# One Trainium2 block kernel: h in a pool of its own, the first residues of pairs on older bytes, h's last squares ahead of its transposes, the third columns' end made prompt

## The chip, the cores and the metric

The kernel runs on one core of one Trainium2 chip. The metric is device time in microseconds (us) of one execution; lower is better. The core has four engines that matter here: TensorE (PE) for matmuls, VectorE (DVE), ScalarE (ACT) and GpSimd (POOL); SyncE (SP) issues most DMAs. Each engine runs its own list of instructions strictly in order. An instruction whose input isn't ready holds up all that stands behind it on that engine.

## What is computed

One layer over 256 tokens of 2048 features: attention heads and a convolution side by side, one output projection that adds into h, then a gated feed-forward network (FFN) that adds into the result. The part around the change is the end of the projection and the start of the FFN:

```python
    mixed = jnp.concatenate([att, u], axis=-1)
    h = h + jnp.einsum('bsm,md->bsd', mixed, w_out[l].astype(mixed.dtype))
    hn = rms_norm(h, norm2_g[l])
    a = jnp.einsum('bsd,df->bsf', hn, w_gate[l].astype(hn.dtype))
    bu = jnp.einsum('bsd,df->bsf', hn, w_up[l].astype(hn.dtype))
    h = h + jnp.einsum('bsf,fd->bsd', jax.nn.silu(a) * bu, w_down[l].astype(hn.dtype))
```

## The kernel before

Products run in a reduced format at float32 accuracy: each operand is the sum of a rounded high part (`hi`) and a residue (`lo`), and a product is made of three matmuls: high by high, residue of the activations by high part of the weights, high part by residue of the weights. For every chunk of weights, SP loads `raw` (512 KB), ACT casts it to `whi` (line 330), and DVE subtracts to get the residue `wlo` (line 339); for some chunks a POOL DMA makes the residue instead. PE uses the high parts first and the residues last.

The program is written as a list of chunks. For each chunk the loads, casts and residues of chunks some places ahead are issued, then its matmuls (`multiply`). What follows a group of chunks (adding a finished sum into h, transposing, normalizing) is written as generators: `multiply` calls `resume()` at fixed places, and each call takes every running generator to its next `yield`. So the number of `yield`s decides behind which chunk's work an instruction stands on its engine. A chunk with `prompt` gets one more `resume()` right after its matmuls if it ends a group.

The output projection has four blocks of 512 columns, n = 0 to 3. The first three are computed with interleaved chunks, and the fourth follows alone. At the end of block n, `out_done(n)` runs: DVE adds the two accumulators into h (line 848, one for each 128 tokens), PE transposes those columns into `ps_h` (line 861), ACT and DVE turn them into `hn` (line 865) or into `chi` and `clo` (870, 872), ACT takes the sums of squares (`h_squares`, line 493), and POOL stores h to DRAM (`h_store`, line 833). "Third columns" are n = 2, "last columns" n = 3. After n = 2, `make_forms` prepares the sums `fhi` and `flo` for the FFN.

The FFN has two kinds of units. Ordinary chunks use `chi` and `clo`. "Pairs" take four weight tiles `wb`, form sums `wt` of them (lines 1038 to 1040; on POOL for the first pair, on DVE for most others), cast both into `wh` (lines 1033, 1055), and take residues `wlb` and `wlt` (line 1062); PE multiplies them by seven products at lines 1078 to 1080.

SBUF is given out by pools that are stacked from both ends. On the right side stand `edge`, `keep` (the two tiles of h, the mixed activations, `junk` for the squares) and `small` (scalars for each row, `rsq` among them). When the last columns are done, `keep` and `small` are closed and the pool `late` takes their bytes: the residues `wlb` and `wlt`, the FFN's sums `sum0` to `sum3`, and others. A tile in `late` waits for whatever last read or wrote the bytes below it.

Of the kernel before, what the change touches and what calls it, by code (L numbers as in the profile page):

```python
# [12 lines left out]
F32 = mybir.dt.float32  # L13
F32R = mybir.dt.float32r
AF = mybir.ActivationFunctionType
ALU = mybir.AluOpType
AX = mybir.AxisListType

P = 128
D = 2048  # L20
S = 256
NM = S // P
# [9 lines left out]
N = 512  # L32
# [3 lines left out]
EPS = 1e-6  # L36
# [95 lines left out]
def tile_block(  # L132
# [6 lines left out]
    act, dve, pool, pe, sp = nc.scalar, nc.vector, nc.gpsimd, nc.tensor, nc.sync  # L139

    const = ctx.enter_context(tc.tile_pool(name="const", bufs=1))
# [4 lines left out]
    prestack, keepstack = ExitStack(), ExitStack()  # L146
    ctx.enter_context(tc.tile_pool(name="edge", bufs=1, side="right")).tile([P, EDGE // 4], F32, tag="edge", name="edge")
    keep = keepstack.enter_context(tc.tile_pool(name="keep", bufs=1, side="right"))
    small = keepstack.enter_context(tc.tile_pool(name="small", bufs=4, side="right"))
    pre = prestack.enter_context(tc.tile_pool(name="pre", bufs=2))  # L150
    acc_ps = ctx.enter_context(tc.tile_pool(name="acc", bufs=4, space=PSUM))
    aux_ps = ctx.enter_context(tc.tile_pool(name="aux", bufs=AUX, space=PSUM))


    h = [keep.tile([P, D], F32, tag=f"h{m}", name=f"h{m}") for m in range(NM)]
    away = ctx.enter_context(tc.tile_pool(name="away", bufs=1, space=bass.MemoryType.DRAM))
    hd = [away.tile([P, D], F32, tag=f"hd{m}", name=f"hd{m}") for m in range(NM)]

# [18 lines left out]
    def col(key, k):  # L177
        return cols[:, AT[key] + k : AT[key] + k + 1]
# [41 lines left out]
        pool.tensor_tensor(neg_lam, le[:, 1:2], le[:, 0:1], ALU.subtract)  # L220
        pool.tensor_scalar(neg_lam, neg_lam, 1.0, -LAMBDA_INIT, ALU.mult, ALU.add)

    def rsqrt_mean(dst, ss, n, eps):

        k = dst.shape[-1]
        t = small.tile([P, 8], F32, tag="rsq", name="rsq")
        pool.tensor_scalar(t[:, :k], ss, 1.0 / n, eps, ALU.mult, ALU.add)
        pool.tensor_tensor(dst, t[:, :k], neghalf[:, :k], ALU.pow)

# [37 lines left out]
    def room(n, hold=0):  # L267
        while held[0] + n > AUX:
            yield
        held[0] += hold  # L270


    side = []
# [21 lines left out]
    chunks = []  # L295
    before = {}

    def block(w, cols, ks, xs, done=None, bkey=None, first=True, last=True, spare=False, cuts=()):

        ks = list(ks)  # L300
        cols = [(cols, N)] if isinstance(cols, int) else cols
        width = sum(n for _, n in cols)
        bkey = bkey if bkey is not None else ("b", len(chunks))
        i = 0
        cuts = list(cuts)
        while i < len(ks):
            part = ks[i : i + (cuts.pop(0) if cuts else NK * N // width)]
            i += len(part)
            chunks.append(dict(w=w, ks=part, k0=part[0], nk=len(part), cols=cols, width=width, xs=xs, bkey=bkey,
                               first=part[0] == ks[0] and first, last=last and i == len(ks),  # L310
                               done=done if i == len(ks) else None, spare=spare, by_dma=False,
                               rows=slice(part[0], part[-1] + 1), load=load_chunk, round=round_chunk,
                               split=split_chunk, multiply=multiply))
# [177 lines left out]
    def square_sum(src, accum, **kw):  # L491
        junk = keep.tile([P, N], F32, tag="junk", name="junk")
        act.activation(junk[:, : src.shape[-1]], src, AF.Square, accum_out=accum, **kw)
# [333 lines left out]
    ss2 = [const.tile([P, 4], F32, tag=f"ss2_{m}", name=f"ss2_{m}") for m in range(NM)]  # L827
    rstd2s = const.tile([P, NM], F32, tag="rstd2", name="rstd2")
    rstd2 = [rstd2s[:, m : m + 1] for m in range(NM)]

    def h_store(cs):
        for m in range(NM):
            pool.dma_start(out=hd[m][:, cs], in_=h[m][:, cs])

    def h_squares(n, cs):
        for m in range(NM):
            square_sum(h[m][:, cs], ss2[m][:, n : n + 1])

    def out_done(n, ps):
        if not n:  # L840
            prestack.close()
            ffn["pool"] = fp = ctx.enter_context(tc.tile_pool(name="ffn", bufs=1))
            ffn["rows"] = fp.tile([P, 2, NS, S], F32, tag="wh", name="hn", bufs=2)
            for t in ("chi", "clo"):
                ffn[t] = fp.tile([P, len(REST), S], F32R, tag=t, name=t)
        cs = slice(n * N, (n + 1) * N)
        for m in range(NM):
            dve.tensor_tensor(h[m][:, cs], h[m][:, cs], ps[m], ALU.add)
        if n == 2:
            held[0] -= NM  # L850
        if n == D // N - 1:
            h_store(cs)
            yield
        yield
        for t in range(0, N // P, 2):
            k = n * (N // P) + t
            yield from room(1)
            pt = aux_ps.tile([P, 2, S], F32, tag="aux", name="ps_h")
            for i in range(2):
                for m in range(NM):  # L860
                    pe.transpose(pt[:, i, m * P : (m + 1) * P], h[m][:, (k + i) * P : (k + i + 1) * P], ident)
            if k % HK < NS:
                rows = ffn["rows"][:, k // HK, k % HK : k % HK + 2, :]
                for i in range(2):
                    act.activation(rows[:, i, :], pt[:, i, :], AF.Copy, scale=col("g2", k + i))
            else:
                a = REST.index(k)
                hi, lo = (ffn[x][:, a : a + 2, :] for x in ("chi", "clo"))
                for i in range(2):
                    act.activation(hi[:, i, :], pt[:, i, :], AF.Copy, scale=col("g2", k + i))  # L870
                for i in range(2):
                    dve.scalar_tensor_tensor(lo[:, i, :], pt[:, i, :], col("g2", k + i), hi[:, i, :].bitcast(F32),
                                             ALU.mult, ALU.subtract)
                    plain[k + i] = (hi[:, i, :], lo[:, i, :])
            yield
        h_squares(n, cs)
        if n < D // N - 1:
            h_store(cs)
        if n == HK * P // N:
            yield  # L880
            start(make_forms())
        if n == D // N - 1:
            yield
            ss = small.tile([P, NM], F32, tag="ssh", name="ssh")
            for m in range(NM):
                dve.tensor_reduce(ss[:, m : m + 1], ss2[m], AX.X, ALU.add)
            rsqrt_mean(rstd2s, ss, D, EPS)
            keepstack.close()
            ffn["late"] = ctx.enter_context(tc.tile_pool(name="late", bufs=1, side="right", reuse_waits="tile"))


    ffn = {}
# [409 lines left out]
    for ks, first, last in ((range(0, 4), True, False), (range(4, 8), False, False), (range(8, 16), False, True)):  # L1302
        for n in range(3):
            block(w_out, n * N, ks, fm, (lambda ps, n=n: out_done(n, ps)) if last else None,
                  bkey=("o", n), first=first, last=last, spare=n == 2)
    block(w_out, 3 * N, range(16), fm, lambda ps: out_done(3, ps))
    chunks[-1]["prompt"] = True
    for i, c in enumerate(chunks[OPENING:-12]):
# [67 lines left out]
```

## Time and profile before

| what | value |
|---|---|
| time, median of 3 runs | 1033.14 us (1032.98 to 1033.17) |
| the profiled execution's own time | 1033.09 us |
| its span in the profile | 1031.3 us |
| DMA moved in the span | 239.71 MB, mean 232 GB/s |
| granted TensorE clock | 1.0 |
| first add into h of the last columns (DVE) | 340.48 us after the span's start |
| first residue of a pair, `wlb` (DVE) | 348.53 us |
| first use of `wlt` (PE) | 352.62 us |

A row of a timeline has the start in us from the span's start, the length, the engine, the line of the kernel, the operation, output and inputs, shapes and count, and in brackets how long the engine idled before it and what ended that. PEld is PE's loading of weights, which runs beside its matmuls.

### The profile page before, as it was taken

What the parts mean: (1) busy time and instruction counts of PE and PEld (TensorE: products, weight loads), DVE (VectorE), ACT (ScalarE), POOL (GpSimd) and SP (SyncE); (2) the same over time, 40 slices, a digit from 0 to 9 for tenths busy, and PEclk for the clock granted to TensorE, in tenths of its full rate; (3) what the DMA queues carried; (4) which work ended last, traced back from release to release, by engine and by line L of the source; (5) the groups of instructions that cost most, each with busy time, mean ns of one, the idle gap of its engine ahead of it and who ended that gap; (6) DMA issues with size and microseconds to landing.
All of it is one profiled execution on the core that took longest, in us unless ns stands there. A gap on an engine that the chain in (4) does not pass through costs nothing.

```text
span 1031.3 us, 13149 instructions
## 1 busy us (share of the span) xinstructions
PE 1023.3 (99%) x4628; PEld 845.4 (82%) x4628; DVE 905.7 (88%) x1160; ACT 668.4 (65%) x863; POOL 185.1 (18%) x193
## 2 busy tenths in 40 slices
PE   9999999999999999999999999999999999999998
PEld 7888888888887778888888888888888888888887
DVE  6899999999756999899988897888989888789897
ACT  7644656665756676777765657677777556767662
POOL 0300112110002100212304212123022231220320
PEclk9999999999999999999999999999999999999999
DMA  9757555545457777987989899889798989797776
GB/s 336 261 189 263 186 184 164 164 163 174 165 191 247 238 226 211 295 268 211 251 261 233 274 286 246 264 239 234 250 276 237 264 228 305 229 259 228 232 189 176
DMA packets 116738, 239.71 MB, mean 232 GB/s; under 512 B 7872, under 2 KB 9152, under 8 KB 116672
## 3 DMA queue, kind: packets, MB, share of 16 engines
q1 hardware_dynamic: 105216, 203.58, 58.7%
q0 software_dynamic: 11168, 35.13, 18.1%
q8 instruction: 36, 0.59, 0.2%
q14 instruction: 30, 0.25, 0.1%
q10 hardware_dynamic: 288, 0.16, 0.1%
HBM read 204.24 MB, written 9.44 MB: 207 GB/s over the span
## 4 chain that ended last, share of the span: by engine, by line
PE 95%; DVE 2%; DMA 1%; issue 0%; SPq 0%; ACT 0%; POOL 0%; DVEq 0%; POOLq 0%; ACTq 0%
PE q L1099 11%; PE q L1100 11%; PE q L1105 11%; PE q L1080 10%; PE acc L375 10%; PE q L1078 10%; PE q L1079 10%; PE acc L369 9%; PE acc L370 9%; PE ps_a L906 1%; DMA wb<-in_w_gate_dram 1%; DMA raw<-in_w_in_dram 1%; DVE wlt L1062 1%; PE ps_s L726 1%; PE ps_o L796 1%; DVE wlb L1062 0%
## 5 line engine op out<-in xcount | busy, mean ns | idle before, releaser
L330 ACT CAST whi<-raw 128x1024 fp32r<-128x1024 f32 (+1 forms) x248 | 257.3, 1044 | 191.0 <-issue 86.4
L339 DVE TENSOR_TENSOR wlo<-raw,whi 128x1024 fp32r<-128x1024 f32 (+1 forms) x198 | 239.2, 1216 | 45.3 <-ACT whi L330 44.9
L1062 DVE TENSOR_TENSOR wlt<-wt,wh 128x1024 fp32r<-128x1024 f32 x130 | 153.0, 1218 | 16.3 <-ACT wh L1055 16.3
L1055 ACT CAST wh<-wt 128x1024 fp32r<-128x1024 f32 x130 | 132.9, 1051 | 41.7 <-DVE wt L1038 28.9
L1099 PE MATMUL q<-whi,chi 128*128 128x512 f32 x352 | 137.8, 391 | 0.0
L1100 PE MATMUL q<-whi,clo 128*128 128x512 f32 x352 | 137.0, 389 | 0.0
L334 POOL DMA_DIRECT2D wlo<-raw x50 | 43.3, 866 | 481.4 <-ACT wlo L333 329.3
L1062 DVE TENSOR_TENSOR wlb<-wb,wh 128x1536 fp32r<-128x1536 f32 x65 | 113.9, 1752 | 17.7 <-ACT wh L1033 16.6
L369 PE MATMUL acc<-whi,xhi 128*128 128x512 f32 x312 | 123.7, 396 | 0.0
L370 PE MATMUL acc<-whi,xlo 128*128 128x512 f32 x312 | 121.7, 390 | 0.0
L1078 PE MATMUL q<-wh,fhi 128*128 128x512 f32 x308 | 120.7, 392 | 0.0
L1079 PE MATMUL q<-wh,flo 128*128 128x512 f32 x308 | 119.9, 389 | 0.0
L586 DVE SCALAR_TENSOR_TENSOR y<-upad,cw,y 128x256 f32<-128x256 f32 x240 | 100.8, 478 | 0.0
L1033 ACT CAST wh<-wb 128x1536 fp32r<-128x1536 f32 x65 | 95.8, 1473 | 4.4 <-DMA wb<-in_w_down_dram 2.4
L1105 PE MATMUL q<-wlo,chi 128*128 128x512 f32 x352 | 94.4, 390 | 0.0
L375 PE MATMUL acc<-wlo,xhi 128*128 128x512 f32 x312 | 84.9, 393 | 0.0
L1105 PEld LDWEIGHTS q<-wlo,chi 128*128 128x128 f32 x352 | 65.8, 188 | 14.4 <-DMA wlo<-raw 0.8
L1099 PEld LDWEIGHTS q<-whi,chi 128*128 128x128 f32 x352 | 66.1, 188 | 13.6
L1100 PEld LDWEIGHTS q<-whi,clo 128*128 128x128 f32 x352 | 66.1, 188 | 13.5
L1099 PE MATMUL q<-whi,ahi 128*128 128x512 f32 x182 | 71.0, 390 | 0.0
L1100 PE MATMUL q<-whi,alo 128*128 128x512 f32 x182 | 70.8, 389 | 0.0
L1080 PE MATMUL q<-wlt,fhi 128*128 128x512 f32 x176 | 68.7, 391 | 1.4 <-DVE wlt L1062 1.4
(247 smaller groups left out, 1845.7 us busy)
## 6 DMA issues: line engine op xcount, KB each, us to landing
raw<-in_w_in_dram SPq DMA_DIRECT2D x78, 512.0 KB, 4.7
wlo<-raw POOLq DMA_DIRECT2D x50, 512.0 KB, 6.3
raw<-in_w_down_dram SPq DMA_DIRECT2D x46, 512.0 KB, 6.5
wb<-in_w_up_dram SPq DMA_DIRECT2D x44, 512.0 KB, 4.3
wb<-in_w_gate_dram SPq DMA_DIRECT2D x44, 512.0 KB, 5.5
raw<-in_w_gate_dram SPq DMA_DIRECT2D x44, 512.0 KB, 5.2
raw<-in_w_up_dram SPq DMA_DIRECT2D x44, 512.0 KB, 5.5
wb<-in_w_down_dram SPq DMA_DIRECT2D x42, 512.0 KB, 5.9
```

Source lines behind the costliest of these rows:

```text
L330: act.copy(c["hi"], c["raw"])
L339: dve.tensor_tensor(c["lo"], c["raw"], c["hi"].bitcast(F32), ALU.subtract)
L369: pe.matmul(ps[m], xhi[:, ms], hi[:, j, :], start=c["first"] and j == 0, stop=False)
L370: pe.matmul(ps[m], xlo[:, ms], hi[:, j, :], start=False, stop=False)
L375: pe.matmul(ps[m], xhi[:, ms], lo[:, j, :], start=False, stop=c["last"] and j == nk - 1)
L1062: dve.tensor_tensor(lo, raw, h.bitcast(F32), ALU.subtract)
L1078: pe.matmul(ps, hi, c["hi"][:, w], start=bool(first), stop=False)
L1079: pe.matmul(ps, lo, c["hi"][:, w], start=False, stop=False)
L1080: pe.matmul(ps, hi, c["lo"][w], start=False, stop=bool(last))
L1099: pe.matmul(ps, xs[i][0][:, ms], hi[:, i, :], start=i == 0 and bool(c["first"].get(qs[m])), stop=False)
L1100: pe.matmul(ps, xs[i][1][:, ms], hi[:, i, :], start=False, stop=False)
L1105: pe.matmul(sum_bank(c, qs[m]), xs[i][0][:, ms], lo[:, i, :], start=False, stop=i == 1 and bool(c["last"].get(qs[m])))
```

## The change

There are four edits. (1) The two tiles of h move from `keep` into a pool `hold` that is opened after `small`, so that it lies at the inner end of the stack. When `late` opens, its tiles `sum0` to `sum3`, `draw` and `dhs` are given out first, ahead of `wlb` and `wlt`. (2) In `out_done` of the last columns, the squares stand ahead of the transposes, and their reduction and `rsqrt_mean` follow one `yield` later, with their small tiles in `const` rather than in `small`. (3) The last chunk of the third columns is marked `prompt`. (4) `out_done` of the third columns has one more `yield` after its adds, which keeps its transposes where they were on PE.

```diff
+    hold = keepstack.enter_context(tc.tile_pool(name="hold", bufs=1, side="right"))
...
-    h = [keep.tile([P, D], F32, tag=f"h{m}", name=f"h{m}") for m in range(NM)]
+    h = [hold.tile([P, D], F32, tag=f"h{m}", name=f"h{m}") for m in range(NM)]
...
-    def rsqrt_mean(dst, ss, n, eps):
+    def rsqrt_mean(dst, ss, n, eps, where=None):
...
-        t = small.tile([P, 8], F32, tag="rsq", name="rsq")
+        t = (where or small).tile([P, 8], F32, tag="rsq", name="rsq")
...
         if n == D // N - 1:
+            h_squares(n, cs)
             h_store(cs)
-            yield
-        yield
+        if n >= 2:
+            yield
+        yield
+        if n == D // N - 1:
+            ss = const.tile([P, NM], F32, tag="ssh", name="ssh")
+            for m in range(NM):
+                dve.tensor_reduce(ss[:, m : m + 1], ss2[m], AX.X, ALU.add)
+            rsqrt_mean(rstd2s, ss, D, EPS, const)
...
-        h_squares(n, cs)
         if n < D // N - 1:
+            h_squares(n, cs)
             h_store(cs)
...
         if n == D // N - 1:
-            yield
-            ss = small.tile([P, NM], F32, tag="ssh", name="ssh")
-            for m in range(NM):
-                dve.tensor_reduce(ss[:, m : m + 1], ss2[m], AX.X, ALU.add)
-            rsqrt_mean(rstd2s, ss, D, EPS)
             keepstack.close()
-            ffn["late"] = ctx.enter_context(tc.tile_pool(name="late", bufs=1, side="right", reuse_waits="tile"))
+            ffn["late"] = late = ctx.enter_context(tc.tile_pool(name="late", bufs=1, side="right", reuse_waits="tile"))
+            for tag, n in (*((f"sum{i}", N) for i in range(4)), ("draw", 4 * N), ("dhs", 2 * N)):
+                late.tile([P, n], F32, tag=tag, name="first")
...
             block(w_out, n * N, ks, fm, (lambda ps, n=n: out_done(n, ps)) if last else None,
                   bkey=("o", n), first=first, last=last, spare=n == 2)
+    chunks[-1]["prompt"] = True
     block(w_out, 3 * N, range(16), fm, lambda ps: out_done(3, ps))
```

The order of PE's instructions is the same as before; those of DVE and ACT change at a few places. The line numbers of the changed kernel are higher by 1 to 8.

On DVE, where the third columns end, the rows are these before (`clo` belongs to the second columns, `acc` is the sum of the third):

```order
L872 SCALAR_TENSOR_TENSOR clo<-ps_h,cols,chi 128x256 x2
L339 TENSOR_TENSOR wlo<-raw,whi 128x1024 x3
L848 TENSOR_TENSOR h_88<-h_88,acc 128x512
L848 TENSOR_TENSOR h_89<-h_89,acc 128x512
L339 TENSOR_TENSOR wlo<-raw,whi 128x1024 x2
L996 SCALAR_TENSOR_TENSOR sums<-hn 128x512
```

And in the changed kernel, on the same engine at the same place:

```order
L880 SCALAR_TENSOR_TENSOR clo<-ps_h,cols,chi 128x256 x2
L340 TENSOR_TENSOR wlo<-raw,whi 128x1024 x2
L849 TENSOR_TENSOR h_91<-h_91,acc 128x512
L849 TENSOR_TENSOR h_92<-h_92,acc 128x512
L340 TENSOR_TENSOR wlo<-raw,whi 128x1024 x3
L1001 SCALAR_TENSOR_TENSOR sums<-hn 128x512
```

The two adds into h have moved ahead of one residue `wlo`.

On ACT, around the end of the last columns, the rows before are (`junk` is written by the squares of h, `wh` is cast for a pair):

```order
L1033 CAST wh<-wb 128x1536
L330 CAST whi<-raw 128x1024
L870 ACTIVATE chi<-ps_h,cols 128x256 x2
L330 CAST whi<-raw 128x1024
L870 ACTIVATE chi<-ps_h,cols 128x256 x2
L493 ACTIVATE junk,ss_0_143<-h_88 128x512
L493 ACTIVATE junk,ss_1_144<-h_89 128x512
L1055 CAST wh<-wt 128x1024 x2
```

The same rows of ACT in the changed kernel:

```order
L1038 CAST wh<-wb 128x1536
L494 ACTIVATE junk,ss_0_146<-h_91 128x512
L494 ACTIVATE junk,ss_1_147<-h_92 128x512
L331 CAST whi<-raw 128x1024
L878 ACTIVATE chi<-ps_h,cols 128x256 x2
L331 CAST whi<-raw 128x1024
L878 ACTIVATE chi<-ps_h,cols 128x256 x2
L1060 CAST wh<-wt 128x1024 x2
```

The two squares now stand ahead of two casts of weights and the four activations that read the transposes.

On DVE behind that, up to the first pair's residues, the rows before are these, with the semaphores that each waits for (DMASW are DMAs that POOL issued, here the eight stores of h):

```order
L339 TENSOR_TENSOR wlo<-raw,whi 128x1024 [waits DMAHW1_49,Activation_49]
L872 SCALAR_TENSOR_TENSOR clo<-ps_h,cols,chi 128x256 [waits PE_49,Activation_49]
L872 SCALAR_TENSOR_TENSOR clo<-ps_h,cols,chi 128x256
L886 TENSOR_REDUCE ssh<-ss_0_143 128x1 [waits Activation_49]
L886 TENSOR_REDUCE ssh<-ss_1_144 128x1 [waits Activation_49]
L1062 TENSOR_TENSOR wlb<-wb,wh 128x1536 [waits DVE_49,Pool_49]
L1062 TENSOR_TENSOR wlt<-wt,wh 128x1024 [waits DMASW4_49,DMASW3_49,DMASW5_49,DMASW2_49,DMASW6_49,DMASW1_49,DMASW7_49,DMASW0_49,Activation_49]
L1062 TENSOR_TENSOR wlt<-wt,wh 128x1024 [waits Activation_49]
```

And in the changed kernel, from the reductions on:

```order
L861 TENSOR_REDUCE ssh<-ss_0_146 128x1
L861 TENSOR_REDUCE ssh<-ss_1_147 128x1
L880 SCALAR_TENSOR_TENSOR clo<-ps_h,cols,chi 128x256 [waits PE_49,Activation_49]
L880 SCALAR_TENSOR_TENSOR clo<-ps_h,cols,chi 128x256
L340 TENSOR_TENSOR wlo<-raw,whi 128x1024 [waits DMAHW1_49,DVE_49,Activation_49]
L880 SCALAR_TENSOR_TENSOR clo<-ps_h,cols,chi 128x256 [waits PE_49,Activation_49]
L880 SCALAR_TENSOR_TENSOR clo<-ps_h,cols,chi 128x256
L1067 TENSOR_TENSOR wlb<-wb,wh 128x1536 [waits Pool_49]
L1067 TENSOR_TENSOR wlt<-wt,wh 128x1024 [waits Activation_49] x2
```

The reductions stand four `clo` and one `wlo` earlier, and the first `wlt` no longer waits for stores of h. The semaphore of POOL that `wlb` still waits for now stands for line 632, a scalar of the convolution's normalization, instead of `rstd` (line 228). The stores of h are waited for later, by the first of the FFN's sums (line 1191 before).

## The prediction

> **What bounds the kernel now.** I read the page's head first, for the size of what can be won at all.
>
> ```profile
> span 1031.3 us, 13149 instructions
> PE 1023.3 (99%) x4628; PEld 845.4 (82%) x4628; DVE 905.7 (88%) x1160; ACT 668.4 (65%) x863; POOL 185.1 (18%) x193
> ```
>
> TensorE (PE) is idle for 8.0 us of 1031.3, and the change takes no matmul away. So only idle time can go. The busy time by stretch says where that is (columns: stretch, length, then busy time and count of PE, PEld, DVE, ACT, POOL, then granted clock, DMA share, GB/s).
>
> ```profile
> 0.00:310.00 310.00, 308.14 (x1427) 255.14 (x1428) 273.23 (x493) 189.08 (x346) 37.82 (x68) 1.00 0.59 204
> 310.00:350.00 40.00, 39.16 (x179) 31.70 (x178) 28.54 (x34) 26.50 (x42) 8.96 (x9) 1.00 0.73 245
> 350.00:380.00 30.00, 28.55 (x124) 22.69 (x123) 29.53 (x30) 20.39 (x20) 1.82 (x2) 1.00 0.78 236
> 380.00:1000.00 620.00, 619.98 (x2777) 513.05 (x2777) 548.70 (x576) 422.30 (x448) 133.09 (x109) 1.00 0.86 248
> 1000.00:1031.30 31.30, 27.52 (x128) 22.84 (x126) 25.68 (x31) 10.17 (x10) 3.43 (x6) 1.00 0.72 184
> ```
>
> The start (1.86 us idle) and the tail (3.78) are not touched. What can be reached lies from 310 to 380: 0.84 and 1.45 us. From 380 to 1000 PE is idle for 0.02 us, so whatever PE gains before 380 is carried to the end. And from 350 to 380 VectorE (DVE) is busy for 29.53 of 30 us: there DVE, not PE, sets the pace. The timeline gives the three stalls. First, the transposes of h's third columns (line 861):
>
> ```profile
> 316.93 1.07 PE L375 MATMUL acc<-wlo,mahi 128*128 128x512 f32 x4
> 318.52 0.30 PE L861 MATMUL ps_h<-ident,h 128*128 128x128 f32 x1 [0.51 <-PE acc L375]
> 319.07 0.55 PE L861 MATMUL ps_h<-ident,h 128*128 128x128 f32 x3 [0.25 <-DVE h L848]
> 319.37 0.47 PE L369 MATMUL acc<-whi,mahi 128*128 128x512 f32 x1
> ...
> 321.30 0.60 PE L861 MATMUL ps_h<-ident,h 128*128 128x128 f32 x4
> 321.65 1.18 PE L375 MATMUL acc<-wlo,mahi 128*128 128x512 f32 x4
> ```
>
> Four matmuls in 1.07, each 0.39 long, start 0.227 apart, so idle time understates a stall by 0.16. The transposes could start at 316.93 + 1.07 - 0.16 = 317.84, and unhindered ones hand over after 0.35 (321.30 to 321.65), at 318.19. The next matmul starts at 319.37: **1.18 us lost**. The other two are the first residues `wlt` of a pair (line 1062):
>
> ```profile
> 352.62 0.50 PE L1080 MATMUL q<-wlt,fhi 128*128 128x512 f32 x1 [0.80 <-DVE wlt L1062]
> ...
> 373.58 0.50 PE L1080 MATMUL q<-wlt,fhi 128*128 128x512 f32 x1 [0.65 <-DVE wlt L1062]
> ```
>
> With 0.16 each, and 0.1 for a first matmul that takes 0.50, they cost 1.06 and 0.91. All three together are 3.15 us: the most that PE could gain here.
>
> **The change, part by part.** The rows around the first stall, on DVE, ScalarE (ACT), POOL and PE:
>
> ```profile
> 314.21 1.07 PE L375 MATMUL acc<-wlo,mchi 128*128 128x512 f32 x4
> 315.51 1.05 ACT L330 CAST whi<-raw 128x1024 fp32r<-128x1024 f32 x1 [2.50 <-DMA raw<-in_w_out_dram]
> 316.59 1.22 DVE L339 TENSOR_TENSOR wlo<-raw,whi 128x1024 fp32r<-128x1024 f32 x1 [2.13 <-ACT whi L330]
> 317.74 1.28 DVE L848 TENSOR_TENSOR h<-h,acc 128x512 f32<-128x512 f32 x2
> 319.65 0.84 ACT L865 ACTIVATE hn<-ps_h,cols 128x256 f32<-128x256 f32 x2 [3.09 <-PE ps_h L861]
> 319.86 2.41 POOL L1038 TENSOR_TENSOR wt<-wb 128x1024 f32<-128x1024 f32 x1
> 321.46 1.90 DVE L339 TENSOR_TENSOR wlo<-raw,whi 128x1024 fp32r<-128x1024 f32 x1 [2.45 <-ACT whi L330]
> 322.35 2.17 POOL L1039 TENSOR_TENSOR wt<-wb,wt 128x512 f32<-128x512 f32 x1
> 324.05 1.04 ACT L330 CAST whi<-raw 128x1024 fp32r<-128x1024 f32 x1
> 324.60 1.30 POOL L1040 TENSOR_TENSOR wt<-wt,wb 128x512 f32<-128x512 f32 x1
> 325.12 1.86 DVE L339 TENSOR_TENSOR wlo<-raw,whi 128x1024 fp32r<-128x1024 f32 x1 [1.75 <-ACT whi L330]
> ```
>
> *Prompt third columns.* The two adds into h stood behind a `wlo` that idled 2.13 us for its cast, which waited 2.50 us for its weights. Now they stand ahead of it and wait for PE alone, whose last third-column matmuls end at 314.21 + 1.07 = 315.28. The adds (1.28) run from about 315.2 to 316.5 in DVE's idle time; the `wlo` still starts at 316.59. They cost nothing, and the transposes at 317.84 find h ready: PE is 1.18 us ahead. The stores of h go out on POOL 2 us sooner, into the same busy DMA stretch.
>
> ACT follows: `hn` at 317.84 + 0.60 = 318.45 instead of 319.65, and what it queues behind that, up to the cast at 324.05, about 1.18 sooner. That cast then ends near 323.9, and the `wlo` of 325.12 can start at 323.95.
>
> *POOL's first sums.* That `wlo` took 1.86 and the one before it 1.90, against 1.22 for the one at 316.59: POOL's lines 1038 to 1040 ran beside both, and POOL's 1039 took 2.17 where 1040 took 1.30. POOL started 0.84 after the adds' end (319.02); now that is 317.3, inside the `wlo` that ends at 317.81, so I start it there: 2.41 + 1.30 + 1.30 and one `wlo` of 1.22 between them end at 324.0. The second `wlo` is all but free of POOL and ends near 325.25 instead of 326.98: DVE is **1.73 us** ahead. Bounds: 1.1 if POOL still meets it, 1.8 if not at all; I take 1.73.
>
> The Trainium skill has a rule on this (SBUF — State Buffer, section Who interferes with whom): a VectorE operation with two SBUF inputs and a GpSimd one that reads SBUF exclude each other for a whole instruction, and whichever issues first makes the other wait. The trace agrees: 1.90 is 1.22 and the 0.8 until POOL's first operation ends at 322.27. By that rule 0.1 us of the 0.64 stays; if both merely slowed each other wherever they touch, all 0.64 could stay, which is the first rival below.
>
> *h's last squares ahead of its transposes, and the residues' new bytes.* The rows of the last columns:
>
> ```profile
> 337.07 3.49 DVE L339 TENSOR_TENSOR wlo<-raw,whi 128x1024 fp32r<-128x1024 f32 x3
> 338.37 1.05 ACT L330 CAST whi<-raw 128x1024 fp32r<-128x1024 f32 x1 [0.35 <-PE acc L370]
> 340.48 1.28 DVE L848 TENSOR_TENSOR h<-h,acc 128x512 f32<-128x512 f32 x2
> 345.75 0.63 ACT L493 ACTIVATE junk<-h 128x512 f32<-128x512 f32 x1
> 345.76 0.40 PE L1099 MATMUL q<-whi,chi 128*128 128x512 f32 x1
> 345.90 0.88 DVE L872 SCALAR_TENSOR_TENSOR clo<-ps_h,cols,chi 128x256 fp32r<-128x256 f32 x2
> 346.69 0.15 DVE L886 TENSOR_REDUCE ssh<-ss 128x1 f32<-128x4 f32 x1
> 347.13 1.98 ACT L1055 CAST wh<-wt 128x1024 fp32r<-128x1024 f32 x2
> 347.26 0.16 DVE L886 TENSOR_REDUCE ssh<-ss 128x1 f32<-128x4 f32 x1 [0.42 <-ACT junk L493]
> 348.53 1.76 DVE L1062 TENSOR_TENSOR wlb<-wb,wh 128x1536 fp32r<-128x1536 f32 x1 [1.12 <-POOL rstd L228]
> 350.21 2.35 DVE L1062 TENSOR_TENSOR wlt<-wt,wh 128x1024 fp32r<-128x1024 f32 x2
> ```
>
> The adds of the last columns come straight behind three `wlo`, so DVE sets their time: 340.48 - 1.73 = 338.75. The squares now stand ahead of the cast of 338.37 on ACT and wait for these adds. The first add ends at 339.45; two squares take 1.38 (345.75 to 347.13); the cast runs from 340.83 to 341.9, 2.5 us later than before. This is the price: DVE, done with the adds at 340.05, idles till 341.9. Then it runs a `wlo` (1.14 from start to start, 337.07 over three), two reductions (0.15 each, partly one under the other, 0.25), two `clo` (0.79, 345.90 to 346.69), a `wlo` (1.14) and two `clo` (0.79), with a little to start each: about 4.15 us, so `wlb` starts at 346.05. Before, it waited for the squares (0.42) and POOL's `rstd` (1.12); both are gone, since the square sums are ready early and its bytes no longer hang on POOL's last reader of the small pool. **348.53 - 346.05 = 2.48 us.** The delayed cast is hidden: its matmuls start at 345.76, now 1.18 sooner at 344.6, and it is ready 2.7 us ahead of them; the cover is gone if the adds come that much later.
>
> The eight stores of h that the first `wlt` waited for cost nothing before: it starts as `wlb` ends (350.21). Moving them to the sums (line 1191, long after) is worth zero. The first `wlt` now ends at 352.56 - 2.48 = 350.08; PE, 1.18 ahead, asks for it at 352.62 - 0.96 - 1.18 = 350.48. The second stall is gone.
>
> *What is late next.* DVE, from there on:
>
> ```profile
> 371.17 2.35 DVE L1062 TENSOR_TENSOR wlt<-wt,wh 128x1024 fp32r<-128x1024 f32 x2
> ```
>
> It ends at 373.52 and PE's third stall ends at 373.58: behind it, PE stands where DVE lets it. DVE has the same work without a gap from 348.53 to there, so that stall stays at its size and the program moves by DVE's 2.48, not by PE's 3.15. I take 2.45 with the rounding. The profiled execution took 1033.09 (span and 1.8 around it; the median of the runs is 1033.14): **1030.6 us**.
>
> **Rivals.** *POOL stays in the way*, or a cast waits for its weights: DVE is then ahead by PE's 1.18 alone, `wlb` starts at 346.6, the gain is 1.9 and the time 1031.2. For it: POOL's end (324.0) and the `wlo` (323.95) almost touch. Against: the DMA share is 0.73 there and no cast but the one at 315.51 waits for weights.
>
> *The adds are not really early*, say because they wait elsewhere. Then the adds of the last columns stay at 340.48, the squares end at 342.55, the cast at 343.6, `wlb` starts at 347.8: gain 0.7, time 1032.4.
>
> *PE, not DVE, decides* (DVE finds a shorter way round the squares): at most 3.15, time 1029.9.
>
> *Slower: the pairs' loads become the bound.* The loads for the third pair go out when the first `wlb` ends, before at 350.3, now 2.45 sooner, nearer to other loads and stores.
>
> ```profile
> 360.27 1.22 DVE L1038 TENSOR_TENSOR wt<-wb 128x1024 f32<-128x1024 f32 x1
> ...
> DMA to landing us min/median/max: 3.5/5.1/11.9
> ```
>
> DVE needs them at 360.27, about 10 us after issue. The second row is for the weights between 300 and 345: up to 11.9 us. At 11.9 the gain falls by 1.9, to 0.5; from 12.5 on it is a loss, and at 14.5 the time is 1035. It takes more than the longest landing seen.
>
> *Nothing changes*: the waits go by other names and PE stands still as long: 1033.
>
> **How the numbers follow.** The forecast (gain 2.1 to 2.9) gets 0.61, POOL in the way 0.15, late adds 0.10, PE deciding 0.06, nothing 0.04, slower 0.04. A measurement here tells 0.2%, 2.1 us, from no change. Faster by that: forecast and PE deciding, 0.67. Slower: 0.04. Within: the rest, 0.29. The range leaves out only nothing, slower and part of PE deciding: from 1029.8 to 1032.4. The forecast's own range is 1030.2 to 1031.0.
>
> **What would show it.** The adds of the third columns ahead of the `wlo` near 315.3 and no idle time before the transposes; a `wlo` near 324 of 1.2 to 1.3; the adds of the last columns near 338.8; a gap of 1.9 on DVE behind them; `wlb` near 346.05 without POOL as releaser; no stall near 350, and one of about 0.65 near 371.1. If `wlb` starts early but the end doesn't move as far, DVE's queue was not the bound behind it, and I am wrong.

## The result and the profile after

| what | before | after |
|---|---|---|
| time, median | 1033.03 us (1032.79 to 1033.17, 6 runs) | 1038.41 us (1037.69 to 1041.21, 5 runs) |
| ratio, after to before | | 1.0056, 95% interval 1.0043 to 1.007 |
| the profiled execution's own time | 1033.09 us | 1038.79 us |
| its span | 1031.3 us | 1037.0 us |

The kernel became slower by 5.4 us, where 2.5 us less had been forecast. (One execution at a granted clock of 0.753 is left out here, 1282.59 us, and one of b_g4 below, 1282.65 us.) The head of the page after, with the counts of its matmuls:

```profile
span 1037.0 us, 13150 instructions
PE 1030.0 (99%) x4628; PEld 847.1 (82%) x4628; DVE 905.4 (87%) x1160; ACT 668.0 (64%) x863; POOL 186.1 (18%) x193
```

PE has the same 4628 instructions, and it is busy for 6.7 us longer. The idle time went from 8.0 to 7.0 us. So the loss isn't waiting: PE is busy for longer with the same matmuls. The busy time by stretch after (columns as in the prediction) says where:

```profile
310.00:350.00 40.00, 40.00 (x185) 32.92 (x183) 30.31 (x37) 29.16 (x45) 10.02 (x10) 1.00 0.77 254
350.00:380.00 30.00, 28.20 (x123) 22.78 (x122) 29.27 (x30) 18.76 (x19) 1.26 (x2) 1.00 0.82 245
380.00:1000.00 620.00, 620.00 (x2753) 508.40 (x2752) 542.33 (x569) 419.73 (x447) 130.04 (x105) 1.00 0.86 247
```

From 310 to 350 PE has no idle time left, as forecast. From 380 to 1000 it is busy throughout and its clock is 1.00, as before, but it gets through 2753 matmuls instead of 2777. At 620 / 2777 = 0.223 us each, 24 matmuls are 5.4 us. Most of the loss is made there, hundreds of microseconds behind the last moved instruction.

The moved instructions themselves do what they were forecast to do. DVE's rows after, at the second, the third and the last columns:

```profile
305.57 1.28 DVE L849 TENSOR_TENSOR h<-h,acc 128x512 f32<-128x512 f32 x2
...
315.73 1.28 DVE L849 TENSOR_TENSOR h<-h,acc 128x512 f32<-128x512 f32 x2 [0.43 <-PE acc L376]
...
324.85 1.23 DVE L340 TENSOR_TENSOR wlo<-raw,whi 128x1024 fp32r<-128x1024 f32 x1 [1.64 <-ACT whi L331]
...
339.62 1.28 DVE L849 TENSOR_TENSOR h<-h,acc 128x512 f32<-128x512 f32 x2
342.80 1.23 DVE L340 TENSOR_TENSOR wlo<-raw,whi 128x1024 fp32r<-128x1024 f32 x1 [1.90 <-ACT whi L331]
...
346.77 1.75 DVE L1067 TENSOR_TENSOR wlb<-wb,wh 128x1536 fp32r<-128x1536 f32 x1
```

The adds wait for PE alone, the `wlo` of 324.85 is free of POOL (1.23), the gap behind the last adds is 1.90, and `wlb` waits for nothing and starts 1.76 us sooner than before. That is not the whole lead. The adds of the second columns, ahead of every moved instruction, stood earlier before:

```profile
304.72 1.28 DVE L848 TENSOR_TENSOR h<-h,acc 128x512 f32<-128x512 f32 x2
```

So the execution after is 0.85 us behind when the changed part begins. (0.45 of it stands already at 25 us; in c_g4 below it is 1.0 at that point, so that much is scatter of the profiled executions.) Counted from these adds, DVE is 1.71 us ahead at the last adds and 2.61 at `wlb`; 1.73 and 2.48 had been forecast.

The waits of PE after (total, times, longest):

```profile
PE q L1110 <- DMA wlo<-raw: 1.8, 1, 1.8
PE ps_warm L169 <- POOL neghalf L163: 1.4, 1, 1.4
```

The waits for `wlt` and for h are gone. A new one has come, for a DMA; its place is in PE's timeline:

```profile
357.11 0.39 PE L1105 MATMUL q<-whi,clo 128*128 128x512 f32 x1
359.31 1.19 PE L1110 MATMUL q<-wlo,chi 128*128 128x512 f32 x4 [1.80 <-DMA wlo<-raw]
```

Two questions follow: why do matmuls that nobody touched run slower, and what became of the time that DVE won?

### The profile page after: what moved, and what is told of

Same layout as the page of the kernel before. It is cut to its first block, busy times and chain, and to the rows that moved or that the text cites. A ratio compares the mean times of both kernels' runs of the same rounds, so it can differ in the third digit from the quotient of the medians.

```text
span 1037.0 us, 13150 instructions
## 1 busy us (share of the span) xinstructions
PE 1030.0 (99%) x4628; PEld 847.1 (82%) x4628; DVE 905.4 (87%) x1160; ACT 668.0 (64%) x863; POOL 186.1 (18%) x193
## 4 chain that ended last, share of the span: by engine, by line
PE 97%; DMA 1%; issue 1%; DVE 0%; ACT 0%; POOL 0%; POOLq 0%; DVEq 0%
PE q L1110 11%; PE q L1104 11%; PE q L1105 11%; PE q L1084 10%; PE q L1085 10%; PE q L1083 10%; PE acc L370 10%; PE acc L371 10%; PE acc L376 10%; DMA wlo<-raw 1%; PE ps_a L911 1%; PE ps_s L727 1%; PE ps_o L797 0%; PE ps_warm L169 0%; PE ps_qk L708 0%
```

## The experiments

### Do the addresses cost?

The change puts two tiles of 32 bytes, `ssh` and `rsq`, into `const`, which lies at the bottom of the left side of SBUF. All that is stacked on the left above it moves up by 64 bytes. In bytes within a partition, by the built programs:

```
            before            after
left  whi    56480  ...        56544     + 64
      chi   126112            126176     + 64
      fhi   150688            150752     + 64
right wlb   179872            200352     + 20480 = 80 x 256
      wlt   192160            212640     + 20480
      sum   208544            179872     - 28672 = 112 x 256
```

Theory A says that the place of the left side against the right costs; B, that the residues' new bytes or the new order cost; C, that a clock lowered by chance does. The first four kernels shift one side or both, with no instruction moved. **b_pad64** is the kernel before with an unused tile:

```diff
     pool.memset(neghalf, -0.5)
+    const.tile([P, 16], F32, tag="pad", name="pad")
```

> The kernel before with one unused 64-byte tile in the constants' pool, so that every tile of the left side lies 64 bytes higher, as in the changed kernel; order, pools and the right side are those of before. Theory A (the addresses: the two small tiles that the change put among the constants shifted the left side from 32 to 96 modulo 128 bytes against a right side at 32, and matmuls from about 245 us on start 0.2295 us apart instead of 0.2270): 1038 to 1040. Theory B (the residues' new bytes above h's old ones, or the new order, slow the matmuls): 1033.0, as before. Theory C (the clock was held back in those executions by chance): 1033, or scattered.

Measured: 1039.75 us (1039.57 to 1040.22), ratio 1.0061 (1.0046 to 1.0076), granted clock 0.999. Sixty-four unused bytes cost as much as the whole change, and more. The stretch of its profile:

```profile
380.00:1000.00 620.00, 620.00 (x2752) 508.36 (x2751) 542.89 (x570) 419.16 (x446) 129.84 (x105) 1.00 0.87 248
```

PE is busy throughout, the clock is 1.00, and there are 2752 matmuls: the same picture as after the change, with the order of before. C falls.

**b_edge** leaves the left side alone and lowers the right one by 64 bytes (before, with `EDGE = 384` for 320):

> The kernel before with the unused tile at the right end larger by 64 bytes: left side at 32 as before, right side at 96 modulo 128. A1 (the difference counts): 1038 to 1040, as with the left side moved. A2 (the left side's own place counts): 1033. Theory B: 1033.

Measured: 1039.64 us (1039.13 to 1040.35), ratio 1.0058 (1.0041 to 1.0075). No left-side tile has moved here and the loss is the same: what counts is the distance of the two sides, not a place of its own.

**a_pad64** and **a_edge** take the changed kernel, one with the same 64-byte tile (left side 128 above that of before), one with `EDGE = 384` (left 64 up, right 64 down): in both the distance has grown by 128.

> The changed kernel with the same 64 unused bytes, so that the left side lies 128 bytes higher than before and both sides are at 32 modulo 128 again. Theory A: matmuls at 0.2270 again and the gain of the order is left, 1030.0 to 1031.5. Theory B: still 1038. Theory C: 1031, or scattered.

> The changed kernel with the unused tile at the right end larger by 64 bytes (384 instead of 320), so that both sides are at 96 modulo 128. If it is the difference of the two sides that counts (theory A1): 1030 to 1031.5. If it is the place of the left side itself (theory A2): still 1038. Theory B: still 1038.

Measured: 1037.82 us (1036.82 to 1038.36) and 1037.52 us (1036.98 to 1038.2), ratios 1.0041 and 1.0039. They agree with each other, which is again the distance, but they are still 4 us slower than before: the distance does not count modulo 128.

### Which distances, and which tiles?

**b_pad32**, **b_pad128** and **b_pad256** are b_pad64 with 8, 32 and 64 floats in the unused tile.

> Before, with the left side 32 bytes up. If the distance of the two sides counts in steps of 64: as before, 1033.2. If any distance other than that of before costs: 1036 to 1040.

> Before, with the left side 128 bytes up instead of 64, nothing else. If what counts is the distance of the two sides modulo 128: as before, 1033.5. If it counts by a larger power of two, or each byte of distance is a new draw: 1036 or more, as with 64.

> Before, with the left side 256 bytes up. If the distance counts modulo 256: as before, 1033.2. If it does not: 1036 to 1040, as with 64 and 128.

Measured: 1040.82 us (ratio 1.0071, 1.0057 to 1.0085), 1038.94 us (1.0057, 1.0042 to 1.0072), and 1033.41 us (0.9999, 0.999 to 1.0008). Thirty-two, 64 and 128 bytes cost 7.6, 6.3 and 5.8 us, and 256 cost nothing. The stretch of b_pad256:

```profile
380.00:1000.00 620.00, 620.00 (x2779) 513.38 (x2778) 549.04 (x577) 423.13 (x449) 133.02 (x109) 1.00 0.87 249
```

With 2779 matmuls it is back at the pace of before.

**b_late64** moves only the FFN's pool on the right (`wlb`, `wlt`, `sum`, `dls`, `dhs`) by 64 bytes:

```diff
+            ctx.enter_context(tc.tile_pool(name="pads", bufs=1, side="right")).tile([P, 16], F32, tag="pad", name="pad")
             ffn["late"] = ctx.enter_context(tc.tile_pool(name="late", bufs=1, side="right", reuse_waits="tile"))
```

> Before, with only the pool of the feed-forward part's right side (wlb, wlt, sum, dls, dhs) 64 bytes lower; the left side, h, mahi and mchi where they were. If a matmul is slowed by the distance of its own two operands: only the matmuls with one operand in this pool (wlb or wlt with fhi, wh with dls or dhs) slow down by 2 to 7 ns, some 500 of 3000, so plus 1 to 3 us. If the distance of anything that moves on the right slows every matmul: as with all of the right side 64 lower, 1039.6. If it is mahi, mchi and the rest of the right side: as before, 1033.2.

Measured: 1039.44 us, ratio 1.006 (1.0046 to 1.0073): the full loss. So it is this pool's distance from the left side that counts in the FFN. Where in the FFN, the starts in PE's timeline tell. The table has the mean time from the start of one 128x512 matmul to the next, in ns, from 345 us on, for three groups. "Pairs" are all matmuls of the pairs; their residues, and in the last product `dls` and `dhs`, are the only operands of these matmuls in the moved pool. The other two groups are ordinary chunks of twelve matmuls, which have both operands on the left: the first chunk behind a pair, and the chunks behind that. (What follows a stall or a transpose, up to the next pair, is left out; some 1330, 670 and 650 of each.)

```
             left side      pairs   first ordinary   later ordinary
           against right            chunk behind     chunks
before            0         227.0       226.7           226.7
after          + 64         230.0       230.1           226.6
b_pad64        + 64         230.0       230.2           226.6
b_edge         + 64         230.0       230.2           226.6
b_late64       + 64         230.0       230.2           226.6
b_pad32        + 32         231.3       228.5           226.9
b_pad128      + 128         230.2       227.7           226.8
a_pad64       + 128         230.2       227.8           226.8
b_pad256      + 256         227.0       226.7           226.8
```

The four kernels at 64 bytes agree to 0.1 ns, whichever side was moved. All of the loss is in the pairs and in the twelve matmuls behind each: in b_late64, 3.0 ns for 1334 and 3.5 for 669 matmuls make 6.3 us, and 6.2 were measured. The later ordinary chunks keep their old pace. (b_pad32 and b_pad128 lose some 0.8 us more between 240 and 310 us, where the projection's activations lie on the right too.)

Why does the first chunk behind a pair lose time, when both its operands lie where they lay? Its times from start to start in b_late64, each a mean over all such chunks, beside those in before behind the stall at 352.62, from the second on:

```
b_late64, behind a pair    228 229 233 236 224 231 236 228 233 231 227
before, behind a stall         229 233 236 224 231 236 228 233 231 226
```

They are the same trail: in both cases PE takes some ten matmuls to find its pace again. (Behind the two shorter stalls of before, near 374 and 508 us, it takes five or six, with the same last times.) So the first chunk doesn't collide with anything itself; it stands behind a disturbance, and the pairs at a wrong distance are one. DVE's instructions beside PE aren't the cause: in b_late64 the first chunk takes 229.8 to 230.4 beside each of DVE's frequent instructions and 230.2 beside an idle DVE, and the later chunks take 226.6 or 226.7 beside the same ones. A conflict between the pairs' own operands on the two sides, with this trail behind it, fits every row. That is read from the traces, not tried: which two accesses meet, and why 256 bytes more are harmless, stays open.

### The change's parts at the old distance

**a_order** has the change's order alone. The two small tiles lie in the unused `edge` tile, h stays in `keep`, and the list of first tiles is left out, so that every tile of the FFN is where it was (only the row scalars in `small`, which are given up before the FFN, lie 128 bytes higher):

```diff
-            ss = const.tile([P, NM], F32, tag="ssh", name="ssh")
+            ss = edge[:, :NM]
...
-            rsqrt_mean(rstd2s, ss, D, EPS, const)
+            rsqrt_mean(rstd2s, ss, D, EPS, edge[:, 8:16])
```

**a_home** is the change with these two lines only, **b_pools** is before with the change's pools only.

> The change's order alone (third columns prompt, h's last squares ahead of its transposes, the wait for rstd moved), with every tile that is not new at its address of before: h stays in the pool keep, the late pool opens without the list of first tiles, and the sums of squares and the reciprocal root's scratch lie in the unused edge tile at the right end. If addresses are all that costs (A, or B in its form of moved bytes): the span falls by the 2.4 us that the prediction gave, about 1030.6, spacing of matmuls as before (0.227 us). If the new order itself costs (B in its form of order): 1036 or more.

> The change as it is, but the two small tiles in the unused edge tile, so that the left side lies where it lay before and only the right side moves (wlb, wlt 20480 bytes up, sums 28672 down). If the left side's 64 bytes are all that costs (A): as the order alone, about 1030.6. If the residues' moved bytes cost too (B, bytes): the wlb and wlt matmuls at 0.234 us as with both sides shifted, and about 1036 to 1038.

> Before, with the change's pools alone: h in hold, the list of first tiles, no step moved; left side as before. A: as before, 1033.5, plus or minus the half microsecond of a changed wait. B, bytes: slower by 4 to 7, 1037.5 to 1040. That would show that of the two moves of addresses each costs by itself.

Measured: a_order 1032.28 us (1030.89 to 1033.62), ratio 0.9989 (0.998 to 0.9998); a_home 1033.12 us (1030.11 to 1034.08), 0.9991 (0.9981 to 1.0001); b_pools 1032.75 us (1031.72 to 1033.4), 0.9996 (0.9987 to 1.0005). The pools cost nothing, and 20480 bytes of move are free as a multiple of 256 is: B falls in both forms. With the left side home the change no longer loses. But it doesn't win 2.45 us either. The longest wait of PE in a_order:

```profile
PE q L1108 <- DMA wlo<-raw: 2.0, 1, 2.0
```

And its windows around that wait (PE busy and count, granted clock, DMA share, GB/s):

```profile
350.00:356.00 6.00, 6.00 (x28) 1.00 0.90 230
356.00:360.00 4.00, 1.97 (x9) 0.97 0.86 267
360.00:364.00 4.00, 4.00 (x13) 0.61 0.86 285
364.00:368.00 4.00, 4.00 (x19) 1.00 0.70 248
```

PE comes to the low half of the third `g` chunk 2.03 us before its DMA has landed, and behind the wait the granted clock falls to 0.61 for four microseconds, in which 13 matmuls run where 19 or 20 would. In the traces of a_order, a_home and a_fix the clock stands at 0.5 for 3.41 us there, which by an estimate costs half of that, 1.7 us. In the ten runs of a_home the four with a mean clock of 0.999 or more take 1030.11 to 1031.73, the six with 0.998 take 1033.0 to 1034.08. The medians are 2.9 apart, more than 1.7, and in a_order two runs with a clock of 1.00 took 1032.65 and 1033.62. So the clock is a part of the loss; the length of the wait, which only a profiled execution shows, is likely another.

### Why the DMA was late

In the first block of the FFN one chunk of each kind gets its residue from an accumulating DMA on POOL's queue. Its line on POOL before, between 340 and 362 us (length in ns, start; who waited for it; time from issue to landing):

```profile
L334 POOL DMA_DIRECT2D wlo<-raw x1: 943/943/943, 351.3 to 351.3; - x1
...
  PEld q L1105: 0.4, 1
...
DMA to landing us min/median/max: 7.6/7.6/7.6
```

And in a_order:

```profile
L335 POOL DMA_DIRECT2D wlo<-raw x1: 943/943/943, 348.6 to 348.6; - x1
...
  PEld q L1108: 2.5, 1
  PE q L1108: 2.0, 1
...
DMA to landing us min/median/max: 10.0/10.0/10.0
```

It is issued 2.7 us sooner and takes 2.4 us longer: it lands at 358.6, against 358.9 before. Before, PE came to it just in time (its weight load waited 0.4 us). The issue moved with DVE and ACT; the landing did not. The DMA share from 350 to 356 is 0.90 in a_order; before it was 0.78:

```profile
350.00:356.00 6.00, 5.20 (x24) 1.00 0.78 215
```

SP's loads of the next pair's weights fall into its flight. In a_order:

```profile
354.47 0.37 SPq L1023 DMA_DIRECT2D wb<-in_w_up_dram  x1
```

And before:

```profile
356.97 0.37 SPq L1020 DMA_DIRECT2D wb<-in_w_up_dram  x1
```

These loads go out when `wlb` frees their buffer, so they come 2.5 us sooner because the residues do. But the accumulating DMA was issued 2.7 us sooner too: the loads stand 5.9 us behind its issue in a_order and 5.7 before, so they have hardly moved against it, and they alone don't tell why it takes longer. The busier DMA share may; that was not tried. In b_prompt, c_squares and after, too, it is issued at 348.8 to 349.9 and lands at 357.8 to 359.2: why the landing stays put is open. That PE's wait for it is what holds the gain was tried. **c_g4** is a_order with the fourth `g` chunk made by DMA instead of the third, so that DVE makes the third's low half and PE asks for the DMA's only one pair of weights later:

```diff
-                   dict(g=TWOS[2:3], u=TWOS[2:3]), swap=not j)
+                   dict(g=TWOS[3:4], u=TWOS[2:3]), swap=not j)
```

**b_g4** is before with the same edit.

> The order alone at the addresses of before (the run of the change's order), with one more edit: in the first block of the feed-forward part the g chunk whose low half an accumulating DMA makes is the fourth, not the third. D (the gain of the order is eaten by the wait of 2.0 us for that DMA, which landed at 358.6 us with the order and at 358.9 before, and by the lower clock that follows the wait): no wait for wlo near 357, granted clock 1.00 from 350 to 380, and the whole gain stays: 1029.5 to 1030.5. E (the order costs somewhere later, the wait only shows it): the wait goes or moves, and the time stays at 1032 to 1033.

> Before with that one edit (the fourth g chunk by DMA in place of the third), order and addresses as before. If the order carries the gain (D): no gain, 1033 to 1034.5, since DVE, which is late from 338 to 357 in before, gets 1.22 us more there. If the edit gains by itself: 1031.

Measured: c_g4 1030.85 us (1030.27 to 1031.61), ratio 0.9977 (0.9967 to 0.9986); b_g4 1033.17 us, 1.0001 (0.9992 to 1.001). The edit gains nothing by itself and 1.4 us with the order; then the order's whole 2.4 us are there. What PE still waits for in c_g4 past 310:

```profile
PE q L1083 <- DVE wlt L1065: 0.8, 1, 0.8
```

This is the stall near 371 that the prediction kept, one residue `wlt` that DVE has late. **a_fix** and **a_fix_g4** give the change as it was made, pools and small tiles included, 192 more unused bytes on the left, without and with that edit:

```diff
     pool.memset(neghalf, -0.5)
+    const.tile([P, 48], F32, tag="pad", name="pad")
```

> The change as it is, with 192 unused bytes more on the left, so that its left side is 256 bytes above that of before. If the distance modulo 256 is all that the change lost by: as the order with the new small tiles in the edge tile, 1030.1 to 1034, median near 1033, with the wait for the accumulating DMA near 357 still there. If the small tiles or the pools cost in another way: 1036 or more.

> The same with the fourth g chunk of the first block by DMA in place of the third. If the wait for the DMA is what eats the order's gain: 1030.5 to 1031, no wait for wlo near 357. If not: as without that edit.

Measured: a_fix 1033.54 us (1030.82 to 1035.73), ratio 0.9998 (0.9989 to 1.0007), with a wait of 2.4 us for the DMA in its profile; the five runs with a clock of 1.00 took 1030.82 to 1031.91. a_fix_g4 1030.86 us (1030.66 to 1031.87), 0.998 (0.9971 to 0.9989). The change loses nothing any more with 192 bytes that nothing uses, and is 0.2% faster than before with one line more.

### Which part of the order carries

**c_g4_noprompt** leaves the prompt third columns out of c_g4. **c_squares** leaves them out of a_order; both keep the change's additional `yield` in the third columns, so they are not the squares alone. **b_prompt** is before with the prompt third columns alone, without that `yield`, by one line:

```diff
+    chunks[-1]["prompt"] = True
     block(w_out, 3 * N, range(16), fm, lambda ps: out_done(3, ps))
```

> The order with the fourth g chunk by DMA (1030.85), without the prompt third columns. If the squares ahead of the transposes carry the gain, as the prediction has it (2.48 of DVE's time, of which 1.73 came from the third columns): 1031 to 1032. If the third columns carry it: 1033.

> Before with the squares ahead of the transposes alone (and the two small tiles in the edge tile), the third g chunk by DMA as before. If its gain is eaten by the wait for that DMA, as with the whole order: 1031 to 1033.5 with a wait of 2 to 3 us near 356, and a granted clock under 1.00 after it. If the squares free DVE early enough without it: 1029.6.

> Before with the prompt third columns alone (one line), all addresses as before. By the prediction's steps (a) and (b): DVE 1.73 us ahead from 325 on, the stalls at 319 gone, so 1031.4 to 1031.9. By the last runs, where leaving them out gained 1.2: 1033 to 1034.5.

Measured: c_g4_noprompt 1029.64 us (1029.48 to 1030.15), ratio 0.9967 (0.9954 to 0.9979), the fastest of all (its runs do not overlap with those of c_g4, the intervals of the two ratios do); c_squares 1030.98 us (1030.35 to 1031.94), 0.9978 (0.9968 to 0.9988); b_prompt 1031.83 us (1031.4 to 1032.46), 0.9987 (0.9978 to 0.9996). The third columns alone gain 1.5 us, with a wait of 1.1 us for the accumulating DMA in the profile; the squares with the `yield` gain 2.3, with two waits of 2.0 in all. Together they gain no more (0.9 in a_order, 2.4 in c_g4), and with the fourth `g` chunk by DMA the prompt third columns cost 1.2 (a_fix_g4, which has them and was run beside c_g4_noprompt, took 1030.86). POOL shows a part of why. Its rows in c_g4:

```profile
316.89 1.14 POOL L834 DMA_DIRECT2D hd<-h  x2 [9.00 <-DVE h L849]
318.05 2.67 POOL L1041 TENSOR_TENSOR wt<-wb 128x1024 f32<-128x1024 f32 x1
```

And in c_g4_noprompt:

```profile
309.14 2.88 POOL L1041 TENSOR_TENSOR wt<-wb 128x1024 f32<-128x1024 f32 x1 [2.23 <-PE ps_h L869]
312.10 1.30 POOL L1042 TENSOR_TENSOR wt<-wb,wt 128x512 f32<-128x512 f32 x1
313.48 2.15 POOL L1043 TENSOR_TENSOR wt<-wt,wb 128x512 f32<-128x512 f32 x1
318.74 1.14 POOL L834 DMA_DIRECT2D hd<-h  x2 [3.11 <-DVE h L849]
```

The change's additional `yield` puts the third columns' work one step back in the program, and so POOL's first sums ahead of the stores of h; they are done by 315.6. Marked prompt, the work comes forward again, the stores stand ahead of the sums on POOL, and the sums run from 318 to 324, beside the `wlo` at 321.33. DVE's last adds and its `wlb` in c_g4:

```profile
321.33 1.84 DVE L340 TENSOR_TENSOR wlo<-raw,whi 128x1024 fp32r<-128x1024 f32 x1 [2.87 <-ACT whi L331]
...
339.81 1.28 DVE L849 TENSOR_TENSOR h<-h,acc 128x512 f32<-128x512 f32 x2
...
346.95 1.75 DVE L1065 TENSOR_TENSOR wlb<-wb,wh 128x1536 fp32r<-128x1536 f32 x1
```

And in c_g4_noprompt, where the `wlo` behind the third columns take 1.23:

```profile
323.53 1.23 DVE L340 TENSOR_TENSOR wlo<-raw,whi 128x1024 fp32r<-128x1024 f32 x1 [3.36 <-ACT whi L331]
...
338.14 1.28 DVE L849 TENSOR_TENSOR h<-h,acc 128x512 f32<-128x512 f32 x2
...
345.28 1.75 DVE L1065 TENSOR_TENSOR wlb<-wb,wh 128x1536 fp32r<-128x1536 f32 x1
```

DVE stands 1.67 us earlier here, but 0.99 of that is scatter: the adds of the second columns start at 305.78 in c_g4 and at 304.79 here, and the two programs are the same up to there. So DVE's times are best counted from those adds. DVE's lead over before, in us:

| | at the last adds | at `wlb` |
|---|---|---|
| forecast | 1.73 | 2.48 |
| after, a_order, c_g4 | 1.71, 1.75, 1.73 | 2.61, 2.66, 2.64 |
| c_squares, c_g4_noprompt | 2.41, 2.41 | 3.32, 3.32 |
| b_prompt | 2.93 | 1.56 |

Up to the last adds c_squares has no moved step but the `yield`, so the 2.41 are the yield's: POOL's sums are out of the way. The squares add 0.9 behind that, in every kernel that has them. In b_prompt DVE comes still earlier to the last adds and then loses 1.37 in the old order. Marking the third columns prompt beside the `yield` costs DVE 0.7 us; PE's wait for the late `wlt` is 0.8 us in c_g4 and 0.3 in c_g4_noprompt. The rest of the 1.2 is not explained by these traces, and no kernel had the `yield` or the squares alone.

In c_squares, two shorter waits for the accumulating DMA (2.0 us in all, 1.1 the longest) stand where a_order has one of 2.0, and the clock stays at 1.00:

```profile
356.00:360.00 4.00, 2.91 (x13) 1.00 0.85 279
360.00:364.00 4.00, 4.00 (x20) 1.00 0.90 284
```

So c_squares keeps 2.3 us where a_order keeps 0.9.

## Why the prediction was wrong, step by step

- **"Only idle time can go"** is the step that failed. It took the time of a matmul as fixed, because the change takes none away, and the edit's two small tiles got no term in the sum. Their 64 bytes on the left cost 6.3 us (b_pad64), and nothing once the left side stood 256 bytes away (a_fix), with every instruction of the change in place: the pairs' matmuls and the chunk behind each went from 227 to 230 ns. "Whatever PE gains before 380 is carried to the end" rested on the same view, and between 380 and 1000 PE got through 24 matmuls fewer without being idle.
- **Prompt third columns.** Right: the adds waited for PE alone, at 315.73 against some 315.2, and the transposes had no idle time before them. In a_order PE is 1.20 us further at 327 than at 310; 1.18 had been forecast. Not seen: that the additional `yield` alone would have brought POOL's first sums ahead of the stores of h, and that marking the columns prompt takes this back.
- **POOL's first sums.** Right in size: 1.71 us of lead at the last adds, counted from the second columns, for 1.73. The second `wlo` was free of POOL (1.23). The first took 2.02 instead of 1.90. The reading that 1.90 is 1.22 and the 0.8 until POOL's operation ends was loose: the two make 2.03, and after the change 1.22 and the 0.94 until the end of POOL's second sum make 2.16 for the 2.02 measured.
- **Squares ahead.** Right: 7.15 us from the last adds to `wlb` (339.62 to 346.77), 7.30 forecast (338.75 to 346.05), with the gap of 1.9 on DVE. In a_order `wlb` starts at 346.05.
- **The pools, at nothing.** Right (b_pools: 0.9996).
- **"What is late next."** Wrong: not the `wlt` near 371, for which PE never waited after the change, but the accumulating DMA at 357. Its issue had moved up with everything else, its landing had not. The rival on the pairs' loads asked the right question, whether a transfer lands in time when its issue moves up, of another transfer.
- **The size.** With the distance kept and the DMA out of the way the order gains 2.4 us (c_g4), and 2.45 had been forecast. The stall on `wlt` is 0.8 us there, where 0.65 had been forecast to stay.

The loss of the change is so told by the experiments: 6.3 us for the 64 bytes (b_pad64), less a gain of the order that the new wait cuts to 0.9 (a_order), agree with the 5.4 that were measured.

## What to carry to other kernels

A change that adds or removes even a small tile moves everything stacked above it: print the tiles' addresses before and after, and keep the distance of the two sides of SBUF at what it was (here modulo 256 bytes, as far as 32, 64, 128 and 256 show it; whether some distance is better than that of before was not tried), or try a few unused bytes as an experiment of its own. When busy time grows and the count of instructions doesn't, compare counts in a stretch without idle time before looking for a wait. When a queue is pulled forward, ask of each transfer that PE needs soon whether its landing moves with its issue. And before comparing times of two profiles, compare a row ahead of the first change: here profiles of the same code differ by up to 1.0 us there.

## What the runs showed of the hardware that was not expected

- The pace of matmuls without any wait depended on the distance of tiles on the two sides of SBUF. Pairs, which read from both sides, took 227.0 ns from start to start at the distance of before and at 256 bytes more, 230.0 at 64 more, 230.2 at 128 and 231.3 at 32.
- PE needed some ten matmuls to come back to its pace, with the same trail (229, 233, 236, 224, 231, 236 ns and so on), behind a stall (before, 352.62) and behind a pair at a wrong distance (b_late64).
- The granted clock fell to half for 3.41 us behind one idle time of PE of 2.0 to 2.4 us (a_order, a_home, a_fix: 0.57 to 0.61 on average from 360 to 364), not behind one of 1.80 (after) nor behind two of which the longer was 1.1 (c_squares). In a_home the clock was 0.998 in 6 of 10 runs, and the median of these is 2.9 us above that of the others. The Trainium skill (TensorE: Matmul & The Clock Gate, part 1 on the HAM clock gate) has the clock go down to half after an idle window of about 3.4 us; here 2.0 us was enough in these profiled executions.
